# Two-tensor operations moved from GpSimd to VectorE in the dense part of a two-block kernel

## The chip, the cores and the metric

The kernel runs on one core of a Trainium2 chip. The metric is the time of one execution on the device in microseconds (us); lower is better. The core has a matrix engine (TensorE, PE in the profile, PEld its weight loads) and three element-wise engines: VectorE (DVE), ScalarE (ACT) and GpSimd (POOL). SyncE (SP) issues most of the transfers (DMA).

## What is computed

Two blocks over 256 tokens of 1024 features, in fp32. The first mixes stick-breaking attention with a state-space branch (S5), attends to a memory of 256 rows, and ends with a feed-forward net with a short convolution. The second mixes an mLSTM with a gated branch and ends with 32 routed experts and a last norm. What the change touches is the norm and the recurrence:

```python
def rms_norm(x, gain):
    y = xf * lax.rsqrt(jnp.mean(xf * xf, axis=-1, keepdims=True) + RMS_EPS)
    return y * gain

def s5_branch(u, a_re, a_im, log_dt, b_re, b_im, c_re, c_im, d_skip, w_glu, b_glu):
    lam_bar = jnp.exp(lam * dt)
    bu = jnp.einsum('gpc,bsgc->bsgp', b_bar, ug)
    _, states = lax.associative_scan(_linear_recurrence_combine, (decay, bu), axis=1)
    y = jnp.einsum('gcp,bsgp->bsgc', c_mat, states).real

h = rms_norm(x, norm_mix_pre)
proj = h @ w_in          # and so on: each dense stage is a norm and products with weights
```

## The kernel before, in words

**Weights.** `Stream` brings each weight matrix in units of 128x1024 elements (512 KB). SP issues the transfer into `wst` (five buffers), ScalarE copies the high part `whi` (L98), and `tick` forms the low part `wlo = wst - whi` on VectorE (L112) or, for the units listed in `gp` or `GU`, on GpSimd (L109). A product with full precision is three TensorE products: high by high, high by low, low by high. A unit makes 24 TensorE products of 256 columns (12 of 512) and four pairs of `whi` and `wlo` rotate.

**Norms.** `norm_by` multiplies the tokens by the gain (`xg`, L279, two pieces of 512), forms the reciprocal root in a chain of eight small VectorE operations on one column (`rs_v`, `rs_y`, `rs_t`, L228 to L238), and puts the root on a diagonal (`diag`, L282). TensorE transposes and scales in one step with it (`ax<-diag,xg`); ScalarE and VectorE split the result into `hT_hi` (L300) and `hT_lo` (L301). There are two tiles `t` of 128 tokens. At a change of stage `post_half` (sum `f`, L864), `post` and `hand_over` end one stage and begin the next with `norm_by`, and `yield_to` says behind which instruction the next units' low parts are ordered, and which of them go to GpSimd (`Y0`, `Y1`, `Y2`).

**State space.** `ssm_params` makes a table `s_T` of the powers of a rotation (cosines and sines) by doubling: on six levels, two products and two sums of growing length (L593, L595, L596), while the angles `s_P` are squared on VectorE (L599 to L601). Then `s_Bp` and `s_C` are built, and for each of four quarters `rotate` (L728 to L731) and `scan` (L737 to L742) run, between 85 and 170 us, with two GpSimd sums each.

**Order.** The program is written as Python that a scheduler orders, engine by engine. `issue_after(x)` puts an instruction behind `x` where both stand on one engine; `self.last["pool"]` is the last sum of the latest scan. At L1109 and L1117 the loads for the memory attention, and at L1314 those for the second block, are issued by GpSimd `behind("pool")`.

Of the kernel before, what the change touches and what calls it, by code (L numbers as in the profile page):

```python
# [14 lines left out]
OP = mybir.AluOpType  # L15
# [13 lines left out]
    return bass.AP(tensor=ap.tensor, offset=ap.offset, ap=[[0, 128], [1, n]])  # L29


GU = (40, 167, 171, 173)


class Stream:


    def __init__(self, k, pool, split, nb, ns, look):
        self.k, self.pool, self.nb, self.look = k, pool, nb, look
        self.plan, self.loaded, self.split, self.low, self.used = [], [], [], [], 0  # L40
        self.free, self.dmas = [], []
        self.limit, self.after, self.first, self.gp = 0, None, None, ()
        self.low_pool = split
        self.more(split, ns, 0)

    def yield_to(self, n, dve, act, pool=(), first=None):

        self.limit, self.after, self.first = self.used + n, (dve, act), first  # L50
        self.gp = [self.used + i for i in pool]

    def behind(self, i, j):
        x = self.first if i < self.limit and j == 0 else self.after and self.after[j]
# [49 lines left out]
    def tick(self):  # L104

        if self.low:
            i, lo, t, hi = self.low.pop(0)
            if i in self.gp or i in GU:
                self.k.nc.gpsimd.tensor_tensor(lo, t, hi, op=OP.subtract)  # L109
            else:  # L110
                with self.behind(i, 0):
                    self.k.nc.vector.tensor_tensor(lo, t, hi, op=OP.subtract)  # L112

    def next(self):
        while len(self.split) < min(len(self.plan), self.used + 1 + self.look):
            while len(self.loaded) <= len(self.split):
                while self.low and len(self.low) >= self.nb:
                    self.tick()
                self.fill()
            if not self._split():  # L120
                break
        self.used += 1
        while self.low and self.low[0][0] < self.used:
            self.tick()
        return self.split[self.used - 1]
# [5 lines left out]
def drive(*gens):  # L131

    gens = list(gens)
    while gens:
        for g in list(gens):
            if next(g, None) is None:
                gens.remove(g)
# [33 lines left out]
class K:  # L171
# [98 lines left out]
    def pair(self, pool):  # L270
        return pool.tile([128, 2], F32, name="ss2", tag="ss2", bufs=6)

    def norm_by(self, pool, t, ss, g, hi, lo, eng=None, dg=None):

        nc = self.nc
        xg = self.xn("xg")
        for n in range(2):
            ns = slice(n * 512, (n + 1) * 512)
            (eng or nc.vector).tensor_tensor(xg[:, ns], self.x[:, t, ns], g[:, ns], op=OP.mult)  # L279
        y = self.rsqrt(pool, ss[:, 0:1], None, ss2=ss[:, 1:2])  # L280
        dg = (dg or pool).tile([128, 128], F32, name="diag", tag="diag", bufs=1)
        self.last["diag"] = nc.vector.tensor_scalar(dg[:], self.ident[:], y[:], None, op0=OP.mult)  # L282
        return self.split_T(xg, hi, lo, t, dg)
# [170 lines left out]
            self.ws.add(w[k * 128:(k + kq) * 128, c0:c0 + ncols], kq, level)  # L454


Y0 = (1, 1)
Y1 = (4,(2,3))
Y2 = (5, (0, 3))


NWARM = 40
# [2 lines left out]
class Block1(K):  # L465
# [56 lines left out]
    def ssm_params(self, pool, work):  # L522
        nc = self.nc
        V, G, A = nc.vector, nc.gpsimd, nc.scalar
# [23 lines left out]
        r = work.tile([128, 16], F32, name="s_r")  # L548
# [32 lines left out]
        T = self.s_T = pool.tile([128, 2, 16, 64], F32, name="s_T")  # L581
# [5 lines left out]
        m4 = tg[:].rearrange("p j e i c -> p j (e i c)").rearrange("p j (a i n) -> p j a i n", a=2, i=16)  # L587
        pm = work.tile([128, 2, 16], F32, name="s_pm")
        for lv in range(8):
            if lv > 1:  # L590
                n = 1 << lv - 2
                for j in range(2):
                    G.tensor_tensor(m4[:, j, :, :, :n], T[:, :, :, :n],  # L593
                                    P[:, lv, j, :][:, None, :, None].to_broadcast([128, 2, 16, n]), op=OP.mult)
                G.tensor_tensor(T[:, 0, :, n:2 * n], m4[:, 0, 0, :, :n], m4[:, 1, 1, :, :n], op=OP.subtract)  # L595
                G.tensor_tensor(T[:, 1, :, n:2 * n], m4[:, 0, 1, :, :n], m4[:, 1, 0, :, :n], op=OP.add)  # L596
            if lv < 7:
                c, s = P[:, lv, 0, :], P[:, lv, 1, :]
                V.tensor_tensor(pm[:], P[:, lv], P[:, lv], op=OP.mult)  # L599
                V.tensor_tensor(P[:, lv + 1, 0, :], pm[:, 0], pm[:, 1], op=OP.subtract)  # L600
                V.scalar_tensor_tensor(P[:, lv + 1, 1, :], c, 2.0, s, op0=OP.mult, op1=OP.mult)  # L601
            yield 1
# [67 lines left out]
    def ssm_scan(self, pool, work, uT, y):  # L670


        nc = self.nc
        V, G, A = nc.vector, nc.gpsimd, nc.scalar
        Bp, C, T, R = self.s_Bp, self.s_C, self.s_T, self.s_R
# [44 lines left out]
        def cs(q):  # L720
            return [T[:, j, 4 * q:4 * q + 4, :].rearrange("p i j -> p (i j)")[:, None, :].to_broadcast([128, 2, 256])
                    for j in range(2)]

        def rotate(q):
            ec, es = cs(q)
            b = bu.pop(q)[:].rearrange("p (a n) -> p a n", a=2)
            m1, m2 = M[q] = [work.tile([128, 2, 256], F32, name=f"s_m{c}", tag=f"s_m{c}", bufs=2) for c in "12"]
            V.tensor_tensor(m1[:], b, ec, op=OP.mult)  # L728
            V.tensor_tensor(m2[:], b, es, op=OP.mult)
            G.tensor_tensor(m1[:, 0], m1[:, 0], m2[:, 1], op=OP.add)  # L730
            G.tensor_tensor(m1[:, 1], m1[:, 1], m2[:, 0], op=OP.subtract)  # L731

        def scan(q):
            ec, es = cs(q)
            m1, m2 = M[q]
            for j in range(2):
                V.tensor_tensor_scan(m2[:, j, :], R[:, 4 * q:4 * q + 4, :].rearrange("p i j -> p (i j)"), m1[:, j, :],  # L737
                                     0.0, op0=OP.mult, op1=OP.add)
            V.tensor_tensor(m1[:], m2[:], ec, op=OP.mult)
            V.tensor_tensor(m2[:], m2[:], es, op=OP.mult)  # L740
            G.tensor_tensor(m1[:, 0], m1[:, 0], m2[:, 1], op=OP.subtract)
            self.last["pool"] = G.tensor_tensor(m1[:, 1], m1[:, 1], m2[:, 0], op=OP.add)  # L742
            for g, h in enumerate(halves):
                A.activation(Cz[h, :, :, g, :], C[h, 1:5, :, 4 * q:4 * q + 4, :].rearrange("p e j i c -> p (e j) i c"),
                             AF.Copy)
# [129 lines left out]
            self.mean2(self.nw, self.x[:, t, ns], s2, n)  # L875
        return s2

    def hand_over(self, t, g, hh, hl, n, pool):

        r = self.norm_by(self.nw, t, self.post(t), g, hh, hl)  # L880
        if t == 0:
            self.diag0 = self.last["diag"]
        else:
            self.ws.yield_to(n, *r, pool, self.diag0)

    def new_h(self):
        return (self.hp.tile([128, 8, 256], F32R, name="hT_hi", tag="hT_hi"),
# [26 lines left out]
    def next_tile(self, t):  # L914
        self.post(t)
# [25 lines left out]
    def block1(self):  # L941
        nc, tc, I = self.nc, self.tc, self.I
        V, G, A = nc.vector, nc.gpsimd, nc.scalar
        c, nw, ws = self.const, self.nw, self.ws
        if True:
# [15 lines left out]
            for nm, n in (("b_gate", 16), ("ssm_d", 4), ("ssm_b_glu", 4)):  # L961
                r = rows[nm] = self.rowp.tile([64, 128], F32, name=f"r_{nm}")
# [17 lines left out]
            hh, hl = self.new_h()  # L980
            for t in range(2):
                ss = self.pair(nw)
                for n in range(2):
                    self.mean2(nw, self.x[:, t, n * 512:(n + 1) * 512], ss, n)
                with self.behind("diag" if t else "const"):
                    r = self.norm_by(nw, t, ss, g, hh, hl, G if t else None, sw if t else None)
            ws.yield_to(Y0[0], *r, range(Y0[1]))

            gT = p1.tile([128, 16, 256], F32, name="gT")
            uT = p1.tile([128, 4, 256], F32, name="uT")  # L990
# [51 lines left out]
            with ExitStack() as s2:  # L1042
                self.banks(3, 0)
                sw = s2.enter_context(tc.tile_pool(name="ssm_work", bufs=1, reuse_waits="tile"))
                a, b = self.stick(nw, qT, kT, v, oh, ol), self.ssm_scan(sp, sw, uT, uT)
# [74 lines left out]
            hh, hl = self.new_h()  # L1120
# [6 lines left out]
            gx = self.gain("norm_xa_pre")  # L1127
# [7 lines left out]
            gp, gx = self.gain("norm_xa_post"), self.gain("norm_ffn_pre")  # L1135
# [50 lines left out]
            oxh, oxl = meh, mel  # L1186
            for h in range(4):
                po = self.bank()
                for dk in range(2):
                    for mt in range(2):  # L1190
# [6 lines left out]
                                op=OP.subtract)  # L1197
            hh, hl = self.new_h()

            drive(self.mode_a(oxh, oxl, 8, 1024, lambda t, b: self.hand_over(t, gx, hh, hl, *Y1), tail=8,  # L1200
                              half=lambda t, n, b: self.post_half(t, n, b, gp)))
            xst.close()

# [1 line left out]
            with tc.tile_pool(name="ffn", bufs=1, reuse_waits="tile") as fp:  # L1205
# [32 lines left out]
                for b in range(6):  # L1238
                    n = 512 if b < 5 else 256
# [8 lines left out]
class Block2(Block1):  # L1248
# [47 lines left out]
        self.h2 = self.new_h()  # L1296

    def next_tile(self, t):
        self.hand_over(t, self.g1, *self.h2, *Y2)

    def plan2(self):
        win = self.I["w_in_2"][0]
# [750 lines left out]
```

## Time and profile before

| | us |
|---|---|
| three runs | 1132.81, 1136.93, 1130.77 |
| their median | 1132.81 |
| the profiled execution | 1129.9 |
| its span, first to last instruction | 1128.2 |
| its mean granted TensorE clock | 0.986 of full speed |
| busy: TensorE, VectorE, ScalarE, GpSimd | 1071.8, 562.6, 439.2, 112.6 |

The dense part (first block, mixer of the second) lasts until some 676 us, then the experts follow. In the rows below a window's columns are its length, the busy time and count of PE, PEld, DVE, ACT and POOL, the granted clock, the share of the 16 DMA engines that moved data, and GB/s. A clock of 0.50 is 1.2 GHz, 1.00 is 2.4 GHz.

### The profile page before, as it was taken

Reading aid. Unit: us, or ns where it says so; the run is one execution under the profiler, and the core shown is the slowest. Engines: PE = TensorE matmul, PEld = TensorE weight load, DVE = VectorE, ACT = ScalarE, POOL = GpSimd, SP = SyncE. Lnnn points to the kernel's source line nnn. Section 1 sums busy time; section 2 is a strip of 40 time slices with the busy share of each in tenths; the row PEclk is TensorE's granted clock in tenths of the full one; section 3 lists DMA queues with packets and bytes.
Section 4 is the critical chain, followed back from the end, with each engine's and each line's share of the span. In section 5 each row is a group of like instructions: output and inputs, shape, how many; then the busy total and the mean of one; then the engine's idle time right before and its main releaser. Section 6 shows DMA issues by size and latency. Waiting matters only on the chain. (4 is left out here: it accounts for less than half of the span.)

```text
span 1128.2 us, 17920 instructions
## 1 busy us (share of the span) xinstructions
PE 1071.8 (95%) x6552; PEld 760.0 (67%) x6552; DVE 562.6 (50%) x1232; ACT 439.2 (39%) x703; POOL 112.6 (10%) x140
## 2 busy tenths in 40 slices
PE   7889999999999999999999879999999999999994
PEld 7878899899887999987798754434343444443332
DVE  8985446995447888855676982211111111211003
ACT  4454467565535766643478331111011101110102
POOL 3734142100002000000101020000000000000000
PEclk9989999999999999999999989999999999999998
DMA  7442255675516665662596676999999999999994
GB/s 225 148 155 91 77 161 182 219 267 162 153 53 222 228 188 171 196 192 80 171 326 239 217 295 246 341 409 409 408 409 409 408 409 372 409 409 408 409 407 157
DMA packets 103850, 294.36 MB, mean 261 GB/s; under 512 B 14733, under 2 KB 17009, under 8 KB 103761
## 3 DMA queue, kind: packets, MB, share of 16 engines
q1 hardware_dynamic: 101136, 286.33, 70.0%
q0 software_dynamic: 2336, 6.35, 1.9%
q8 instruction: 52, 0.85, 0.3%
q10 hardware_dynamic: 288, 0.52, 0.1%
q14 instruction: 38, 0.30, 0.1%
HBM read 304.70 MB, written 1.05 MB: 271 GB/s over the span
## 5 line engine op out<-in xcount | busy, mean ns | idle before, releaser
L112 DVE TENSOR_TENSOR wlo<-wst,whi 128x1024 fp32r<-128x1024 f32 x171 | 213.9, 1259 | 98.9 <-ACT whi L98 97.8
L98 ACT ACTIVATE whi<-wst 128x1024 fp32r<-128x1024 f32 x180 | 188.1, 1057 | 131.7 <-PE mm L194 116.3
L194 PE MATMUL mm<-hT_hi,wlo 128*128 128x256 f32 x672 | 190.3, 283 | 6.7 <-DVE wlo L112 6.7
L194 PE MATMUL mm<-hT_hi,whi 128*128 128x256 f32 x672 | 193.8, 289 | 0.0
L194 PE MATMUL mm<-hT_lo,whi 128*128 128x256 f32 x672 | 190.0, 283 | 0.0
L194 PEld LDWEIGHTS mm<-hT_hi,wlo 128*128 128x128 f32 x672 | 128.3, 191 | 7.1 <-DVE wlo L112 7.1
L194 PEld LDWEIGHTS mm<-hT_hi,whi 128*128 128x128 f32 x672 | 128.2, 191 | 1.7 <-issue 1.4
L194 PEld LDWEIGHTS mm<-hT_lo,whi 128*128 128x128 f32 x672 | 128.3, 191 | 0.2
L1683 DVE SCALAR_TENSOR_TENSOR hid<-gu,ws,hid 128x512 f32<-128x512 f32 x16 | 12.0, 751 | 228.3 <-PE gu L1677 228.3
L1691 ACT ACTIVATE hidT<-yd 128x512 f32<-128x512 f32 x16 | 9.6, 598 | 157.0 <-PE yd L207 157.0
L109 POOL TENSOR_TENSOR wlo<-wst,whi 128x1024 fp32r<-128x1024 f32 x9 | 22.5, 2506 | 365.8 <-DVE rs_y L238 175.2
L1711 DVE SCALAR_TENSOR_TENSOR ylo<-gu,ws,yhi 128x512 fp32r<-128x512 f32 x16 | 12.0, 751 | 89.2 <-ACT yhi L1710 89.2
L194 PE MATMUL mm<-whi,hT_hi 128*128 128x512 f32 x128 | 51.5, 410 | 2.8 <-DVE f L864 2.8
L194 PE MATMUL mm<-whi,hT_lo 128*128 128x512 f32 x128 | 51.3, 404 | 0.0
L194 PE MATMUL mm<-wlo,hT_hi 128*128 128x512 f32 x128 | 51.1, 403 | 0.0
L1682 ACT ACTIVATE hid<-gt,ws 128x512 f32<-128x512 f32 x16 | 11.0, 687 | 102.0 <-PE gt L1677 102.0
L1710 ACT ACTIVATE yhi<-gu,ws 128x512 fp32r<-128x512 f32 x16 | 11.0, 687 | 99.1 <-PE gu L1701 99.1
L1987 POOL TENSOR_TENSOR o<-o,go 128x512 f32<-128x512 f32 x2 | 2.5, 1265 | 448.6 <-ACT o L1986 448.6
L1677 PE MATMUL gu<-xr,x 128*64 128x512 f32 x112 | 38.3, 596 | 1.4 <-DMA xr<-in_w_up_dram 1.4
L1677 PE MATMUL gu<-ra,x 128*64 128x512 f32 x140 | 35.3, 597 | 0.8 <-DMA ra<-in_w_up_dram 0.6
L194 PE MATMUL mm<-whi,ah 128*128 128x512 f32 x88 | 34.8, 396 | 0.0
L194 PE MATMUL mm<-wlo,ah 128*128 128x512 f32 x88 | 34.8, 395 | 0.0
(607 smaller groups left out, 2288.1 us busy)
## 6 DMA issues: line engine op xcount, KB each, us to landing
wst<-in_w_in_dram SPq DMA_DIRECT2D x56, 512.0 KB, 4.6
wst<-in_ffn_w_up_dram SPq DMA_DIRECT2D x44, 512.0 KB, 4.5
ra<-in_w_gate_dram SPq DMA_DIRECT2D x35, 512.0 KB, 9.9
ra<-in_w_up_dram SPq DMA_DIRECT2D x35, 512.0 KB, 10.1
ra<-in_w_down_dram SPq DMA_DIRECT2D x30, 512.0 KB, 10.1
xr<-in_w_up_dram SPq DMA_DIRECT2D x28, 512.0 KB, 7.0
xr<-in_w_down_dram SPq DMA_DIRECT2D x26, 512.0 KB, 10.1
xr<-in_w_gate_dram SPq DMA_DIRECT2D x24, 512.0 KB, 10.1
```

The costliest lines, as they stand in the source:

```text
L98: nc.scalar.activation(hi[:, :m], t[:, :m], AF.Copy)
L109: self.k.nc.gpsimd.tensor_tensor(lo, t, hi, op=OP.subtract)
L112: self.k.nc.vector.tensor_tensor(lo, t, hi, op=OP.subtract)
L194: i = self.nc.tensor.matmul(out, lhsT=lhsT, rhs=rhs, start=start, stop=stop, skip_group_check=True)
L1677: self.nc.tensor.matmul(ps[r, :], lhsT=xe[:, k, e], rhs=w[g][k], start=k == 0, stop=k == 7, skip_group_check=True)
L1682: self.nc.scalar.activation(hid[:], ps_g[:], AF.Silu, scale=y)
L1683: self.nc.vector.scalar_tensor_tensor(hid[:], ps_u[:], y, hid[:], op0=OP.mult, op1=OP.mult)
L1691: self.nc.scalar.activation(hT[:].rearrange("p a b -> p (a b)"), ps[:], AF.Copy)
L1710: self.nc.scalar.activation(hi[:], ps[n][:], AF.Copy, scale=ws)
L1711: self.nc.vector.scalar_tensor_tensor(lo[:], ps[n][:], ws, hi[:].bitcast(F32), op0=OP.mult, op1=OP.subtract)
L1987: G.tensor_tensor(o[1, n][:], o[1, n][:], self.go[:, ns], op=OP.mult)
```

## The change

Every two-tensor operation that GpSimd did in the dense part stands on VectorE: the gain product of the second tile in the first norm (2), the products and sums of the rotation table (24), the sums of `rotate` and `scan` (16), and nine low parts, one in the first norm, two each at two stage changes, four by `GU`. The arithmetic is the same.

```diff
-GU = (40, 167, 171, 173)
...
-    def yield_to(self, n, dve, act, pool=(), first=None):
+    def yield_to(self, n, dve, act, first):
         self.limit, self.after, self.first = self.used + n, (dve, act), first
-        self.gp = [self.used + i for i in pool]
...
             i, lo, t, hi = self.low.pop(0)
-            if i in self.gp or i in GU:
-                self.k.nc.gpsimd.tensor_tensor(lo, t, hi, op=OP.subtract)
-            else:
-                with self.behind(i, 0):
-                    self.k.nc.vector.tensor_tensor(lo, t, hi, op=OP.subtract)
+            with self.behind(i, 0):
+                self.k.nc.vector.tensor_tensor(lo, t, hi, op=OP.subtract)
...
-    def norm_by(self, pool, t, ss, g, hi, lo, eng=None, dg=None):
+    def norm_by(self, pool, t, ss, g, hi, lo, dg=None):
...
-            (eng or nc.vector).tensor_tensor(xg[:, ns], self.x[:, t, ns], g[:, ns], op=OP.mult)
+            nc.vector.tensor_tensor(xg[:, ns], self.x[:, t, ns], g[:, ns], op=OP.mult)
...
-Y0 = (1, 1)
-Y1 = (4,(2,3))
-Y2 = (5, (0, 3))
+Y0, Y1, Y2 = 1, 4, 5
...
                 for j in range(2):
-                    G.tensor_tensor(m4[:, j, :, :, :n], T[:, :, :, :n],
+                    V.tensor_tensor(m4[:, j, :, :, :n], T[:, :, :, :n],
                                     P[:, lv, j, :][:, None, :, None].to_broadcast([128, 2, 16, n]), op=OP.mult)
-                G.tensor_tensor(T[:, 0, :, n:2 * n], m4[:, 0, 0, :, :n], m4[:, 1, 1, :, :n], op=OP.subtract)
-                G.tensor_tensor(T[:, 1, :, n:2 * n], m4[:, 0, 1, :, :n], m4[:, 1, 0, :, :n], op=OP.add)
+                V.tensor_tensor(T[:, 0, :, n:2 * n], m4[:, 0, 0, :, :n], m4[:, 1, 1, :, :n], op=OP.subtract)
+                V.tensor_tensor(T[:, 1, :, n:2 * n], m4[:, 0, 1, :, :n], m4[:, 1, 0, :, :n], op=OP.add)
...
-            G.tensor_tensor(m1[:, 0], m1[:, 0], m2[:, 1], op=OP.add)
-            G.tensor_tensor(m1[:, 1], m1[:, 1], m2[:, 0], op=OP.subtract)
+            V.tensor_tensor(m1[:, 0], m1[:, 0], m2[:, 1], op=OP.add)
+            V.tensor_tensor(m1[:, 1], m1[:, 1], m2[:, 0], op=OP.subtract)
...
-            G.tensor_tensor(m1[:, 0], m1[:, 0], m2[:, 1], op=OP.subtract)
-            self.last["pool"] = G.tensor_tensor(m1[:, 1], m1[:, 1], m2[:, 0], op=OP.add)
+            V.tensor_tensor(m1[:, 0], m1[:, 0], m2[:, 1], op=OP.subtract)
+            self.last["pool"] = V.tensor_tensor(m1[:, 1], m1[:, 1], m2[:, 0], op=OP.add)
...
-    def hand_over(self, t, g, hh, hl, n, pool):
+    def hand_over(self, t, g, hh, hl, n):
...
-            self.ws.yield_to(n, *r, pool, self.diag0)
+            self.ws.yield_to(n, *r, self.diag0)
...
-                    r = self.norm_by(nw, t, ss, g, hh, hl, G if t else None, sw if t else None)
-            ws.yield_to(Y0[0], *r, range(Y0[1]))
+                    r = self.norm_by(nw, t, ss, g, hh, hl, sw if t else None)
+            ws.yield_to(Y0, *r, self.last["diag"])
```

The lines of the changed kernel have numbers lower by 8 to 10 (L112 is L104 there, L282 is L274, L301 is L293, L593 is L583, L864 is L854).

**The order at the start.** On VectorE, from the first tile's diagonal on, in the kernel before:

```order
L282 TENSOR_SCALAR diag<-ident,rs_y 128x128
L228 SCALAR_TENSOR_TENSOR rs_v<-ss_246 128x1
L229 TENSOR_SCALAR rs_y<-rs_v 128x1
L234 SCALAR_TENSOR_TENSOR rs_t<-rs_y,rs_v 128x1
L238 SCALAR_TENSOR_TENSOR rs_y<-rs_t,rs_y 128x1
L234 SCALAR_TENSOR_TENSOR rs_t<-rs_y,rs_v 128x1
L238 SCALAR_TENSOR_TENSOR rs_y<-rs_t,rs_y 128x1
L234 SCALAR_TENSOR_TENSOR rs_t<-rs_y,rs_v 128x1
L238 SCALAR_TENSOR_TENSOR rs_y<-rs_t,rs_y 128x1
L282 TENSOR_SCALAR diag<-ident,rs_y 128x128
L301 TENSOR_TENSOR hT_lo<-ax,hT_hi 128x4x128 x3
```

and in the changed kernel:

```order
L274 TENSOR_SCALAR diag<-ident,rs_y 128x128
L271 TENSOR_TENSOR xg<-x,gbc 128x512 x2
L220 SCALAR_TENSOR_TENSOR rs_v<-ss_246 128x1
L221 TENSOR_SCALAR rs_y<-rs_v 128x1
L226 SCALAR_TENSOR_TENSOR rs_t<-rs_y,rs_v 128x1
L230 SCALAR_TENSOR_TENSOR rs_y<-rs_t,rs_y 128x1
L226 SCALAR_TENSOR_TENSOR rs_t<-rs_y,rs_v 128x1
L293 TENSOR_TENSOR hT_lo<-ax,hT_hi 128x4x128
L230 SCALAR_TENSOR_TENSOR rs_y<-rs_t,rs_y 128x1
L226 SCALAR_TENSOR_TENSOR rs_t<-rs_y,rs_v 128x1
L293 TENSOR_TENSOR hT_lo<-ax,hT_hi 128x4x128
L230 SCALAR_TENSOR_TENSOR rs_y<-rs_t,rs_y 128x1
```

The second tile's two gain products stand behind the first diagonal now, and the first low part (`wlo_0_85`, a few rows further on, behind the second diagonal) ahead of the third `hT_lo`.

On GpSimd, from the IOTA that both have early, in the kernel before:

```order
L651 IOTA s_gi 128x8
L279 TENSOR_TENSOR xg<-x,gbc 128x512 x2
L109 TENSOR_TENSOR wlo_0_85<-wst,whi_0_84 128x1024
L538 COPY s_tv<-s_c 128x4x64 x4
L647 COPY s_R<-s_r_773 128x1024
L648 MEMSET s_R 128x16
L593 TENSOR_TENSOR s_tg<-s_T,s_P 128x32 x2
L595 TENSOR_TENSOR s_T<-s_tg 128x16
L596 TENSOR_TENSOR s_T<-s_tg 128x16
```

and in the changed kernel:

```order
L641 IOTA s_gi 128x8
L1251 DMA bif<-in_b_igate_dram 4x1
L1251 DMA bif<-in_b_fgate_dram 4x1
L459 DMA rows<-in_conv_qk_dram 8x128 x2
L320 DMA gbc<-in_norm_mem_dram 128x1024
L1815 DMA wr<-in_w_router_group_dram 128x8x4
L1816 DMA wr<-in_w_router_expert_dram 128x8x32
L1820 DMA brow<-in_b_router_group_dram 128x4 x2
L320 DMA gbc<-in_norm_mix_post_dram 128x1024
L1821 DMA brow<-in_b_router_expert_dram 128x32
L528 COPY s_tv<-s_c 128x4x64 x4
L637 COPY s_R<-s_r_773 128x1024
```

The loads that stood behind the last scan sum (in the trace of before at 152.5 us and later) stand ahead of the copies of `s_c` now, since that sum is on another engine.

**The order in the table.** On VectorE, from the end of the table to unit 12's low part (the `wlo` in the last row), in the kernel before:

```order
L112 TENSOR_TENSOR wlo_1_87<-wst,whi_1_86 128x1024
L662 TENSOR_TENSOR s_tv<-s_Bp,s_lam 128x512 x2
L667 TENSOR_TENSOR s_Bp<-s_tv 128x256 x2
L112 TENSOR_TENSOR wlo_2_89<-wst,whi_2_88 128x1024
L662 TENSOR_TENSOR s_tv<-s_Bp,s_lam 128x1024 x2
L112 TENSOR_TENSOR wlo_3_91<-wst,whi_3_90 128x1024
L667 TENSOR_TENSOR s_Bp<-s_tv 128x256 x4
L112 TENSOR_TENSOR wlo_0_85<-wst,whi_0_84 128x1024
```

and in the changed kernel:

```order
L104 TENSOR_TENSOR wlo_2_89<-wst,whi_2_88 128x1024
L624 TENSOR_TENSOR s_Bp<-s_Bp,s_tv 128x256
L625 TENSOR_TENSOR s_Bp<-s_Bp,s_tv 128x256
L104 TENSOR_TENSOR wlo_3_91<-wst,whi_3_90 128x1024
L652 TENSOR_TENSOR s_tv<-s_Bp,s_lam 128x512 x2
L1007 COPY bgate<-ax 128x16
L657 TENSOR_TENSOR s_Bp<-s_tv 128x256 x2
L1007 COPY dskip<-ax 128x4
L652 TENSOR_TENSOR s_tv<-s_Bp,s_lam 128x1024 x2
L1007 COPY bglu<-ax 128x4
L657 TENSOR_TENSOR s_Bp<-s_tv 128x256 x4
L104 TENSOR_TENSOR wlo_0_85<-wst,whi_0_84 128x1024
```

In the changed kernel the low parts of units 10 and 11 (`wlo_2_89`, `wlo_3_91`) stand ahead of the long products with `s_lam`, and that of unit 12 (`wlo_0_85`) behind all `s_Bp`. In the kernel before, units 10 and 11 stand between these products. The table's products and sums stand among the rows ahead of these.

**The order at the stage change at 532 us.** On VectorE, from the second tile's half of `f` on (L864, L854 in the changed kernel), in the kernel before:

```order
L238 SCALAR_TENSOR_TENSOR rs_y<-rs_t,rs_y 128x1
L282 TENSOR_SCALAR diag<-ident,rs_y 128x128
L112 TENSOR_TENSOR wlo_1_87<-wst,whi_1_86 128x1024
L112 TENSOR_TENSOR wlo_0_2313<-wst,whi_0_2312 128x1024
L301 TENSOR_TENSOR hT_lo<-ax,hT_hi 128x4x128 x2
L112 TENSOR_TENSOR wlo_2_2317<-wst,whi_2_2316 128x1024
L864 TENSOR_TENSOR f<-mm,gbc 128x512
L228 SCALAR_TENSOR_TENSOR rs_v<-ss_5604 128x1
L229 TENSOR_SCALAR rs_y<-rs_v 128x1
```

and in the changed kernel:

```order
L230 SCALAR_TENSOR_TENSOR rs_y<-rs_t,rs_y 128x1
L274 TENSOR_SCALAR diag<-ident,rs_y 128x128
L104 TENSOR_TENSOR wlo_0_85<-wst,whi_0_84 128x1024
L104 TENSOR_TENSOR wlo_1_87<-wst,whi_1_86 128x1024
L293 TENSOR_TENSOR hT_lo<-ax,hT_hi 128x4x128 x2
L104 TENSOR_TENSOR wlo_0_2313<-wst,whi_0_2312 128x1024
L104 TENSOR_TENSOR wlo_1_2315<-wst,whi_1_2314 128x1024
L854 TENSOR_TENSOR f<-mm,gbc 128x512
L220 SCALAR_TENSOR_TENSOR rs_v<-ss_5604 128x1
L104 TENSOR_TENSOR wlo_2_2317<-wst,whi_2_2316 128x1024
L221 TENSOR_SCALAR rs_y<-rs_v 128x1
```

Where two low parts stood between the diagonal and `hT_lo` and one behind, now two stand in each place, and a fifth behind `rs_v`.

## Rows read from the trace of the kernel before

**Rows 1.** Page, part 1: busy us (share of the span) xinstructions of each engine.
```profile
PE 1071.8 (95%) x6552; PEld 760.0 (67%) x6552; DVE 562.6 (50%) x1232; ACT 439.2 (39%) x703; POOL 112.6 (10%) x140
```

**Rows 2.** Busy time by stretches of the span, core 0.
```profile
28.00:56.00 28.00, 25.06 (x213) 24.70 (x212) 27.86 (x87) 13.35 (x20) 20.90 (x25) 1.00 0.46 148
60.00:66.00 6.00, 5.25 (x23) 5.20 (x24) 6.00 (x10) 1.88 (x5) 4.23 (x5) 0.50 0.56 170
544.00:546.00 2.00, 2.00 (x6) 1.52 (x5) 1.89 (x6) 0.60 (x2) 0.00 (x0) 0.50 0.89 305
676.00:682.00 6.00, 4.73 (x36) 4.55 (x36) 3.60 (x20) 2.85 (x14) 0.00 (x0) 0.92 0.00 0
```

**Rows 3.** Groups by shape on DVE, 169 to 190 us, where GpSimd does nothing.
```profile
L112 DVE TENSOR_TENSOR wlo<-wst,whi 128x1024 fp32r<-128x1024 f32 x6 | 7.2, 1222 | 3.8 <-ACT whi L98 3.8
L1074 DVE TENSOR_TENSOR mg<-mm,gT 128x256 f32<-128x256 f32 x4 | 1.4, 418 | 4.4 <-ACT gT L1071 4.4
...
L234 DVE SCALAR_TENSOR_TENSOR rs_t<-rs_y,rs_v 128x1 f32<-128x1 f32 x3 | 0.7, 221 | 0.1
```

**Rows 4.** Timeline of the start: start, length, instruction, [idle before <-releaser].
```profile
9.57 2.48 POOL L279 TENSOR_TENSOR xg<-x,gbc 128x512 f32<-128x512 f32 x2 [6.13 <-DMA x<-in_x_dram]
9.61 1.24 DVE L234 SCALAR_TENSOR_TENSOR rs_t<-rs_y,rs_v 128x1 f32<-128x1 f32 x1
...
10.88 1.19 DVE L238 SCALAR_TENSOR_TENSOR rs_y<-rs_t,rs_y 128x1 f32<-128x1 f32 x1
...
12.02 2.34 POOL L109 TENSOR_TENSOR wlo<-wst,whi 128x1024 fp32r<-128x1024 f32 x1
12.11 2.27 DVE L234 SCALAR_TENSOR_TENSOR rs_t<-rs_y,rs_v 128x1 f32<-128x1 f32 x1
...
15.39 5.17 PE L194 MATMUL ax<-diag,xg 128*128 128x128 f32 x32 [5.75 <-DVE diag L282]
```

**Rows 5.** Timeline of the rotation table: DVE and POOL.
```profile
35.41 0.53 POOL L593 TENSOR_TENSOR s_tg<-s_T,s_P 128x32 f32<-128x32 f32 x2 [2.71 <-DVE s_P L601]
...
50.36 4.83 POOL L593 TENSOR_TENSOR s_tg<-s_T,s_P 128x1024 f32<-128x1024 f32 x2
...
50.48 2.93 DVE L112 TENSOR_TENSOR wlo<-wst,whi 128x1024 fp32r<-128x1024 f32 x1
...
53.33 5.16 DVE L662 TENSOR_TENSOR s_tv<-s_Bp,s_lam 128x1024 f32<-128x1024 f32 x2
...
61.95 1.22 DVE L112 TENSOR_TENSOR wlo<-wst,whi 128x1024 fp32r<-128x1024 f32 x1
```

**Rows 6.** Timeline of TensorE: where units 10, 11 and 12 begin or wait.
```profile
53.47 0.38 PE L194 MATMUL mm<-hT_hi,wlo 128*128 128x256 f32 x1 [2.94 <-DVE wlo L112]
...
60.74 0.58 PE L194 MATMUL mm<-hT_hi,wlo 128*128 128x256 f32 x1 [3.71 <-DVE wlo L112]
...
65.61 0.58 PE L194 MATMUL mm<-whi,hT_hi 128*128 128x512 f32 x1
```

**Rows 7.** Timeline of the stage change at 532 us: DVE, POOL and PE.
```profile
532.17 2.40 DVE L234 SCALAR_TENSOR_TENSOR rs_t<-rs_y,rs_v 128x1 f32<-128x1 f32 x1
...
532.20 2.36 POOL L109 TENSOR_TENSOR wlo<-wst,whi 128x1024 fp32r<-128x1024 f32 x1 [175.16 <-DVE rs_y L238]
...
535.14 2.05 PE L194 MATMUL ax<-diag,xg 128*128 128x128 f32 x16 [2.28 <-DVE diag L282]
...
539.76 2.55 DVE L112 TENSOR_TENSOR wlo<-wst,whi 128x1024 fp32r<-128x1024 f32 x1 [1.20 <-ACT whi L98]
...
542.97 0.50 PE L194 MATMUL mm<-whi,hT_hi 128*128 128x512 f32 x1 [2.77 <-DVE f L864]
```

**Rows 8.** Timeline inside the mLSTM: DVE and PE.
```profile
624.84 2.44 DVE L236 TENSOR_TENSOR rs_t<-rs_y 128x4 f32<-128x4 f32 x2
...
628.73 0.30 PE L207 MATMUL ax<-ident,so 128*128 128x128 f32 x1 [1.61 <-DVE so L1405]
```

**Rows 9.** DMA queues, 152 to 163 us: packets, MB, share of 16 engines.
```profile
q0 software_dynamic: 591, 1.23, 43.3%
```

More of the change, by code (lines that the diff above doesn't have):

```diff
@@ L41, in __init__ @@
         self.free, self.dmas = [], []
-        self.limit, self.after, self.first, self.gp = 0, None, None, ()
+        self.limit, self.after, self.first = 0, None, None
         self.low_pool = split
         self.more(split, ns, 0)
-    def yield_to(self, n, dve, act, pool=(), first=None):
+    def yield_to(self, n, dve, act, first):
         self.limit, self.after, self.first = self.used + n, (dve, act), first
-        self.gp = [self.used + i for i in pool]
     def behind(self, i, j):
@@ L1198, in block1 @@
             hh, hl = self.new_h()
-            drive(self.mode_a(oxh, oxl, 8, 1024, lambda t, b: self.hand_over(t, gx, hh, hl, *Y1), tail=8,
+            drive(self.mode_a(oxh, oxl, 8, 1024, lambda t, b: self.hand_over(t, gx, hh, hl, Y1), tail=8,
                               half=lambda t, n, b: self.post_half(t, n, b, gp)))
@@ L1298, in next_tile @@
     def next_tile(self, t):
-        self.hand_over(t, self.g1, *self.h2, *Y2)
+        self.hand_over(t, self.g1, *self.h2, Y2)
     def plan2(self):
```

## The prediction

> **What bounds the kernel now.** I read the page's first part, then the busy time by stretches, then the timeline at each stretch where TensorE stands idle. TensorE is busy 1071.8 of 1128.2 us and GpSimd 112.6 [rows 1]: the sum over the whole span says only that TensorE leads, so the change is worth what TensorE's pauses ahead of the experts are worth. The stretches [rows 2] (length; busy time of PE, PEld, DVE, ACT, POOL, each with its count; granted clock; DMA share; GB/s) show where these lie. From 28 to 56 us VectorE is busy 27.86 of 28 and GpSimd 20.90, while TensorE has 25.06. From 676 to 682 the DMA share is 0.00: the stream of expert weights starts afresh there, released by the routing behind the dense part, so what the dense part gains should reach the end.
>
> Undisturbed, a low part of 128x1024 takes VectorE 1222 ns, a two-input operation of 128x256 418 ns, one step of the root 221 ns [rows 3]. Through two points that is 0.15 us and 1.05 ns for each element, and the next one starts some 0.08 us before the end of the one ahead (my estimate from starts in the timeline).
>
> **Part one, the start.** While GpSimd multiplies the second tile's gain from 9.57 and forms the first low part from 12.02, VectorE's root steps of one element for each partition take 1.24 and 2.27 us where 0.22 is usual; TensorE stands 5.75 us for the diagonal [rows 4]. These two steps and the one of 1.19 us between them hold an excess of 1.02 + 2.05 + 1.0 = 4.1 us. Without GpSimd the diagonal comes so much earlier. VectorE gets two products of 128x512 (0.61 us each) and one low part (1.14) instead, 2.4 us; they stand behind the first diagonal, and the first tile's products (half of 5.17 us) cover all but some 0.9. Best case: 3.2 us.
>
> The order shows a side effect. The DMA issues that GpSimd held back behind its last scan sum now stand right behind `s_gi`, some 150 us earlier, at about 3.4. In the stretch 152 to 163 us this queue moved 1.23 MB and took 43.3% of the 16 engines for 11 us [rows 9], which is 4.8 us of all engines. At the start these engines are filled with `x`, the gain and the first weights. If all of it lands ahead of what TensorE waits for, more than the 3.2 is gone; but the second large row waits for VectorE's second gain product, and the small ones behind it, so rather a third to a half counts. I take a gain of 1.7 and keep 0 to 3.2.
>
> **Part two, the rotation table.** Here 24 operations move. Their sizes are 2 x (32+64+...+1024) for the products and 2 x (16+...+512) for the sums, 6048 elements in all: 6048 x 1.05 ns + 24 x 0.07 us = 8.0 us on VectorE [rows 3]. Each reads what the one ahead wrote, and I add 1 us for that, and 0.3 us for three copies that now stand ahead: 9.3.
>
> Against it stands what VectorE loses to GpSimd. From 35.41, where the table begins, to the end of unit 12's low part (61.95 + 1.22 = 63.17) [rows 5] it executes, by the order, 26 operations of 16 or 32 elements, 4 of 512, 8 of 256 and 8 of 1024, one behind the other. Undisturbed these are 26 x 0.085 + 4 x 0.61 + 8 x 0.34 + 8 x 1.14 = 16.5 us; it took 27.8. The excess of 11.3 us lies in rows such as the low part of 2.93 us, and 5.16 us for two products whose undisturbed time is 2.4, under two GpSimd products of 4.83 [rows 5]. So the low part of unit 12 ends at 63.17 - 11.3 + 9.3 = 61.2, and with the start 59.5.
>
> Is it the shared way to SBUF? The rows show VectorE slowed and GpSimd too. The Trainium skill (SBUF — State Buffer, section Who interferes with whom) goes further: a VectorE instruction with two SBUF inputs and a GpSimd instruction that reads SBUF exclude each other for the whole instruction. By that rule VectorE would lose nearly all of GpSimd's time in the table, about 20 us rather than 11, and the change would free twice as much. The trace agrees at the root steps and not here, where VectorE finished a low part and half a product under GpSimd's two; I go by the 11.3.
>
> For TensorE: it now waits 2.94 us for unit 10's low part and 3.71 for unit 11's, and then runs at half clock (granted 0.50 from 60 to 66) [rows 2, 6], so unit 12 starts at 65.61 and not at 63.5. After the change units 10 and 11 have their low parts ahead of most of the `s_Bp` work, and unit 12 behind it. From unit 10's low part to unit 12's there are 8.8 us of VectorE work, so unit 10's ends at 50.7. TensorE would be there at 50.5 - 1.7 = 48.8, waits 1.9, is through unit 11 at 56.4, and waits 3.1 for unit 12 at 59.5. That is 6.1 us ahead of 65.61; if this pause brings the low clock as the one of 3.71 did, 2 us less. **I take 4.5 us for parts one and two; bounds 0 (start gains nothing, half the excess stays, clock drops) and 7.5.**
>
> **Part three, the stage change at 532 us.** A root step takes 2.40 us beside GpSimd's low part of 2.36, and TensorE waits 2.28 for the diagonal; then a low part of 2.55 us on VectorE stands ahead of the sum `f` beside GpSimd's second, and TensorE waits 2.77 for `f` [rows 7], and has the low clock (0.50) from 544 to 546 [rows 2]. After the change no GpSimd work is there. The two low parts stand on VectorE behind the diagonal (order below) and cost 2.3 us. The diagonal then comes 2.2 us earlier, and its wait goes. `f` is queued behind four low parts, two before and two behind `hT_lo`, and the last two must wait for ScalarE's high parts; it starts at about 538.8 rather than 542.3, and TensorE, which is there at 542.97 - 2.77 - 2.2 = 538.0, waits 1.5 rather than 2.77. The low clock cost some 8 products 0.19 us each (starts in the timeline), 1.5 us, and a pause of 1.5 should not bring it. Sum 2.2 + 1.2 + 1.5 = 4.9; if ScalarE delays the last low part by more, or the clock falls all the same, 2.2. **I take 4.8, bounds 2.2 and 5.5.**
>
> **Part four, the rest.** At 628.73 TensorE waits 1.61 us for VectorE's `so`, just after two root steps of 2.44 us beside GpSimd [rows 8]; these fall back to 0.2, and of the two low parts that VectorE gets for it (2.3 us) one lies earlier: **1 us, bounds -1 and 2**. The 16 rotation and scan sums (0.34 us each, 5.4 in all) go to VectorE between 85 and 170 us, in which it is idle over half of the time; each chain gets shorter, since GpSimd took over 0.7 us for each and a hand-over. Low parts at 193, 339 and 596 us lie where TensorE did not wait for them. **0, bounds -1 and 1.**
>
> **Sum.** 4.5 + 4.8 + 1 = 10.3 us off the profiled execution's 1129.9 (span 1128.2 and 1.7 around it) is 1119.6. The median of the three runs, 1132.8, is 2.9 above that execution, so I forecast 1122 for a median.
>
> **Rivals.**
> *VectorE becomes the bound (slower).* It is full in the table already, gets 9.3 us there, and TensorE waits for its low parts. If the long rows were VectorE's own chain of dependent small operations, unit 12's low part would come at 63.17 + 9.3 = 72.5, 6.9 us behind 65.61, and with the clock and 1 us at each of two stage changes it is +9 to +11: 1143. It decides once less than about 6 of the 11.3 us vanish. Against it: the long rows are long for single instructions of a known size, and only beside GpSimd. The Trainium skill (Perfetto Trace Analysis, section Optimizing Scalar/DVE Operations) advises giving work away from a saturated VectorE, which would speak against this change, and adds that GpSimd may not help because of the shared port. The trace bears out the second half: 2.40 us beside 2.36. Chance 0.07.
>
> *The early DMAs eat the gain.* If they delay `x`, the first weights and then `s_c` by the full 4.8 us, the start loses 1.6 instead of gaining 1.7, and TensorE's transposes of `s_tv` come late: parts one and two give 0 to 1, the sum is some 5, the median 1128. For it: the engines are full then. Chance 0.16.
>
> *The experts swallow it.* Their weights stream at full DMA load to the end; if that stream's start is fixed by loads and not by routing, the time stays at 1131 to 1133. Against it: the 0.00 from 676 to 682 [rows 2]. Chance 0.05.
>
> **How the numbers follow.** The forecast has 0.72. Its own range is 1129.9 less 15.5 (all upper bounds) to less 5, with the 2.9: 1117 to 1128. For 8 in 10 I add the early DMAs and part of the swallowed case: 1115 to 1130. About 0.5% (5.7 us) is what a measurement here can tell from no change. Faster than 1127.1: nearly all of the forecast and a little of the second rival, 0.74; same: most of the second and the third, 0.19; slower: 0.07.
>
> **What would show it.** In the changed kernel's profile no root step longer than 0.3 us at 9 to 16 and 532; VectorE's low parts at 36 to 62 back to 1.22 us; TensorE's first product at 17 to 20 us instead of 20.4, its wait for unit 11 gone and one of about 3 us at unit 12; at the stage change no wait for the diagonal and at most 1.5 for `f`. Wrong would be: first product after 20.4 (DMAs), VectorE rows that stay long without GpSimd, a wait at unit 12 of over 6 us, or a routing that ends 10 us earlier while the last store does not.

## The result and the profile after

The changed kernel takes 1116.5 us (median of 4 runs, 1115.6 to 1118.7) against 1131.8 before: a ratio of 0.9864, 95% interval 0.9841 to 0.9887. Run once more later, beside other kernels, it had 0.989 (0.9869 to 0.991). It is faster by 12 to 15 us; the forecast was 1122 with a range of 1115 to 1130, and a gain of 10.3 us. Since the changed kernel's own ratio moved by 0.003 from the first group of runs to the last, differences of 2 to 3 us between kernels of different groups below rest on their traces, and those within a group on the times too. Two traces of the changed kernel itself agree within 0.2 us from 62 to 180 us and lie 2.1 to 2.8 us apart from 270 us on, so a difference of that size late in a trace shows nothing by itself.

The page's first part, in the columns of [rows 1]:

```profile
PE 1068.7 (96%) x6552; PEld 756.5 (68%) x6552; DVE 565.6 (51%) x1283; ACT 438.7 (39%) x703; POOL 54.6 (5%) x89
```

GpSimd lost 58 us of busy time and VectorE gained 3. The work that moved is more than 3 us on VectorE; what it no longer loses beside GpSimd makes up for the rest. The stretch that had 27.86 us of VectorE and 20.90 of GpSimd [rows 2] shows it:

```profile
28.00:56.00 28.00, 24.04 (x182) 23.69 (x181) 26.21 (x106) 13.87 (x21) 2.12 (x3) 0.88 0.53 182
```

VectorE executes 106 instructions instead of 87 there. Nearly all of the 1.8 us in which it is idle are a wait for weights (below); behind that it is as full as before, 25.91 of 26 us from 36 to 62. TensorE has less than before (24.04 against 25.06), at a mean clock of 0.88: a new pause lies in this stretch (below).

Where the time came from is read by comparing the start of the same TensorE instruction in both traces; the difference is what has been gained up to there.

| TensorE instruction | before | after | gained |
|---|---|---|---|
| first product with weights | 20.36 | 17.26 | 3.1 |
| unit 12, first product with a low part | 66.02 | 62.08 | 3.9 |
| first product behind the state space's first block | 87.32 | 81.53 | 5.8 |
| behind the second wait for `uT` | 129.92 | 122.72 | 7.2 |
| second tile's transposes, stage change at 532 | 535.14 | 525.67 | 9.5 |
| first product of the next stage | 542.97 | 532.29 | 10.7 |
| the same stage, at full clock again | 547.41 | 535.19 | 12.2 |
| experts, a transpose at 697 us | 697.26 | 683.80 | 13.5 |
| end of the span | 1128.2 | 1114.0 | 14.2 |

**The start**, in the timeline (start, length, instruction, idle before and its releaser), answers to [rows 4]:

```profile
10.04 0.22 DVE L226 SCALAR_TENSOR_TENSOR rs_t<-rs_y,rs_v 128x1 f32<-128x1 f32 x1
...
10.94 0.28 DVE L274 TENSOR_SCALAR diag<-ident,rs_y 128x128 f32<-128x128 f32 x1
...
11.28 2.05 PE L186 MATMUL ax<-diag,xg 128*128 128x128 f32 x16 [2.08 <-DVE diag L274]
...
15.44 2.02 PE L186 MATMUL ax<-diag,xg 128*128 128x128 f32 x16 [2.11 <-DVE diag L274]
...
28.63 1.06 ACT L93 ACTIVATE whi<-wst 128x1024 fp32r<-128x1024 f32 x1 [5.85 <-DMA wst<-in_w_in_dram]
...
29.72 1.23 DVE L104 TENSOR_TENSOR wlo<-wst,whi 128x1024 fp32r<-128x1024 f32 x1 [4.13 <-ACT whi L93]
```

The root steps are back at 0.22 us and the diagonal is there at 10.94 instead of 15.05. TensorE then waits 2.11 us for the second diagonal (forecast 0.9), and the clock makes up for that: its 32 transposes take 4.1 us, and took 5.17 before, where the granted clock from 15 to 20 us was 0.68. The last two rows show what the late loads below prove to be the price of GpSimd's early loads: the weights of unit 5 land late, ScalarE waits 5.85 us for them and VectorE 4.13.

**The table and unit 12**, timeline, beside [rows 5, 6]:

```profile
45.53 2.34 DVE L583 TENSOR_TENSOR s_tg<-s_T,s_P 128x1024 f32<-128x1024 f32 x2
...
47.89 1.21 DVE L104 TENSOR_TENSOR wlo<-wst,whi 128x1024 fp32r<-128x1024 f32 x1
...
49.15 0.58 PE L186 MATMUL mm<-hT_hi,wlo 128*128 128x256 f32 x1 [3.96 <-DVE wlo L104]
...
62.08 0.50 PE L186 MATMUL mm<-wlo,hT_hi 128*128 128x512 f32 x1 [0.87 <-DVE wlo L104]
```

The low part takes 1.21 us, the two longest products 2.34 (forecast at the rate of 1.05 ns an element: 2.3). But the 4.13 us in which VectorE had no weights come back as a wait of 3.96 at unit 9. It stands where the forecast had no wait, and the one forecast at unit 12 is 0.87 and not 3.1.

**The stage change** at 532 us, timeline, beside [rows 7]:

```profile
525.33 0.29 DVE L274 TENSOR_SCALAR diag<-ident,rs_y 128x128 f32<-128x128 f32 x1
525.53 2.36 DVE L104 TENSOR_TENSOR wlo<-wst,whi 128x1024 fp32r<-128x1024 f32 x2
...
531.55 0.69 DVE L854 TENSOR_TENSOR f<-mm,gbc 128x512 f32<-128x512 f32 x1 [0.20 <-ACT sq L260]
...
532.29 0.50 PE L186 MATMUL mm<-whi,hT_hi 128*128 128x512 f32 x1 [1.56 <-DVE f L854]
```

No wait for the diagonal, 1.56 us for `f` (forecast 1.5), and no low clock behind it (granted 1.00 from 532 to 538).

### The profile page after: what moved, and what is told of

Its sections match the earlier page's. It is cut to its first block, busy times and chain, and to the rows that moved or that the text cites. A ratio compares the mean times of both kernels' runs of the same rounds, so it can differ in the third digit from the quotient of the medians.

```text
span 1114.0 us, 17908 instructions
## 1 busy us (share of the span) xinstructions
PE 1068.7 (96%) x6552; PEld 756.5 (68%) x6552; DVE 565.6 (51%) x1283; ACT 438.7 (39%) x703; POOL 54.6 (5%) x89
## 3 DMA queue, kind: packets, MB, share of 16 engines
HBM read 304.70 MB, written 1.05 MB: 274 GB/s over the span
## 5 line engine op out<-in xcount | busy, mean ns | idle before, releaser
L104 DVE TENSOR_TENSOR wlo<-wst,whi 128x1024 fp32r<-128x1024 f32 x180 | 220.5, 1235 | 98.0 <-ACT whi L93 97.2
L186 PE MATMUL mm<-whi,al 128*128 128x512 f32 x88 | 34.7, 396 | 0.0
L1667 PE MATMUL gt<-ra,x 128*64 128x512 f32 x140 | 33.5, 596 | 0.6 <-DMA ra<-in_w_gate_dram 0.6
```

The source lines that it names most:

```text
L186: i = self.nc.tensor.matmul(out, lhsT=lhsT, rhs=rhs, start=start, stop=stop, skip_group_check=True)
L1667: self.nc.tensor.matmul(ps[r, :], lhsT=xe[:, k, e], rhs=w[g][k], start=k == 0, stop=k == 7, skip_group_check=True)
```

## The experiments

Ratios are to the kernel before, from runs on the same chip. The first four ran as one group, the next four as a second, the last three as a third.

**Late loads.** Is the early issue of GpSimd's loads a cost, and how large?

```diff
-            self.last["pool"] = V.tensor_tensor(m1[:, 1], m1[:, 1], m2[:, 0], op=OP.add)
+            V.tensor_tensor(m1[:, 1], m1[:, 1], m2[:, 0], op=OP.add)
...
-                G.tensor_copy(um[h, :, r, :], ...)
+                self.last["pool"] = G.tensor_copy(um[h, :, r, :], ...)
```

> The changed kernel, but GpSimd's loads for the memory attention and the second block stay behind a GpSimd copy of the last quarter of the scan, as late as in the kernel before. Theory A (VectorE gains by GpSimd's silence, and the early loads are a cost): unit 5's weights land some 4 us earlier, VectorE no longer stands idle 4.13 us ahead of that low part, TensorE's wait of 3.96 us at unit 9 and the low clock behind it go; 3 to 6 us below the changed kernel, 1110 to 1114. Rival B (the early loads are part of the gain, since they no longer run beside weights at 152 us): the gain shrinks, 1117 to 1121. Rival C (they don't matter): 1116 to 1117.

Measured: 1119.9 us, 0.9893 (0.9871 to 0.9914), above the changed kernel's first 0.9864 and level with its second 0.989. The total lies in rival B's range; the trace does not speak for it. Unit 12's first low product is at 59.10, 3.0 us earlier than in the changed kernel, as theory A says. Then that gain is lost in one place, and TensorE is 1.7 us behind the changed kernel at 85 us. It stays 1.7 behind up to 200 us, so the loads that run beside weights at 152 us cost nothing there. The timeline on GpSimd, VectorE and TensorE, and the busy time by stretches (in the columns of [rows 2]):

```profile
58.93 14.89 POOL L677 COPY s_Bz<-s_Bp 64x512 f32<-64x512 f32 x1
...
73.26 0.56 DVE L807 SCALAR_TENSOR_TENSOR at<-az,at 128x384 f32<-128x384 f32 x1
...
75.48 0.90 PE L199 MATMUL sb<-ident,s_Bz 128*128 128x128 f32 x3 [3.15 <-POOL s_Bz L677]
```

```profile
76.00:78.00 2.00, 2.00 (x9) 1.91 (x8) 0.00 (x0) 1.11 (x2) 1.84 (x4) 0.50 0.81 212
58.00:74.00 16.00, 13.24 (x64) 10.88 (x64) 16.00 (x25) 8.04 (x13) 15.92 (x3) 1.00 0.60 198
```

A copy that takes GpSimd 1.6 us in the changed kernel (and 0.7 in a later quarter) took 14.89. Through these 16 us VectorE was busy without a gap, and its rows there have their undisturbed lengths (a low part 1.22 us). GpSimd came through only when VectorE's row of operations with two inputs in SBUF broke off: the copy ends at 73.82, with the operation of 0.56 us that reads one of its two inputs (`az`, which TensorE writes) from PSUM. TensorE waited 3.15 us for it, and its clock fell to 0.50 behind the wait.

**The sums back on GpSimd.**

```diff
-            V.tensor_tensor(m2[:], m2[:], es, op=OP.mult)
-            V.tensor_tensor(m1[:, 0], m1[:, 0], m2[:, 1], op=OP.subtract)
-            self.last["pool"] = V.tensor_tensor(m1[:, 1], m1[:, 1], m2[:, 0], op=OP.add)
+            self.last["pool"] = V.tensor_tensor(m2[:], m2[:], es, op=OP.mult)
+            G.tensor_tensor(m1[:, 0], m1[:, 0], m2[:, 1], op=OP.subtract)
+            G.tensor_tensor(m1[:, 1], m1[:, 1], m2[:, 0], op=OP.add)
...  (and the two sums of rotate)
```

> The changed kernel with the 16 sums of rotate and scan on GpSimd again, and the loads left early. Theory A: TensorE's two waits for uT come back (0.5 and 0.75 us, with what they move 1.4), the wait of 1.5 for the transposed block does not, since it hung on s_Bp: 1117.5 to 1118.5. Rival (all that was gained between 66 and 130 us, 3.3 us, is due to these sums): 1119.5 to 1120.5. Rival (hidden): 1116.5.

Measured: 1119.6 us, 0.9883 (0.9862 to 0.9905), between the changed kernel's two ratios, so the total tells nothing. What TensorE waited for between 60 and 170 us in its profiled execution (total, times, longest):

```profile
PE sb L199 <- POOL s_Bz L677: 3.2, 1, 3.2
PE mm L186 <- DVE wlo L104: 1.8, 1, 1.8
PE yq L702 <- DVE uT L748: 1.3, 2, 0.8
```

The two waits for `uT` are back and cost 1.4 us in the trace, as theory A has it. The first row is the shut-out copy again (14.90 us); this execution took 1124.4 and the three others 1118.6 to 1120.0. That suits a copy that is shut out in some executions of one kernel and not in others, but the three have no trace, so it is not shown.

**The table back on GpSimd**, alone and on the best version below.

```diff
-                    V.tensor_tensor(m4[:, j, :, :, :n], T[:, :, :, :n],
+                    G.tensor_tensor(m4[:, j, :, :, :n], T[:, :, :, :n],
...  (and the two sums below)
```

> The changed kernel with the 24 products and sums of the rotation table on GpSimd again. Theory A (what VectorE loses beside GpSimd is more than the work it takes over): VectorE's rows at 36 to 62 us are long again, unit 12 starts 2 to 5 us later and the wait for the transposed block (1.5) comes back: 1119 to 1124. Rival B (the 3.96 us wait at unit 9 is VectorE's own work, so the table is better off on GpSimd): 1112 to 1116.

Measured: 1126.6 us, 0.9947 (0.9929 to 0.9966), 6.5 to 9 us above the changed kernel by its two ratios, and 8.8 in the trace at 82 us, more than theory A expected; rival B is out. VectorE's low part for unit 12 starts 2.5 us later, and TensorE's first product with it 4.5 us later. TensorE's waits from 28 to 100 us:

```profile
PE mm L186 <- DVE wlo L104: 8.5, 4, 4.4
PE sb L186 <- ACT s_BT L688: 2.3, 1, 2.3
```

**The low parts alone**, moved in the kernel before.

```diff
-GU = (40, 167, 171, 173)
+GU = ()
...
-Y1 = (4,(2,3))
-Y2 = (5, (0, 3))
+Y1 = (4,())
+Y2 = (5, ())
```

> The kernel before with only the eight later low parts on VectorE (units 40, 167, 171, 173 and those of the two stage changes); start, table and sums stay on GpSimd. Theory A: the waits for the diagonal (2.28) and for f (2.77 to 1.5) and the low clock (1.5) at 532 us go, and 1 us in the mLSTM: 6 us below before, 1125 to 1127. Rival (the gain at 532 comes from the shifted arrival of weights, not from GpSimd): 1129 to 1132.

Measured: 1127.6 us, 0.994 (0.9914 to 0.9965): 6 to 7 us off. Between 525 and 560 us one wait of TensorE is left, the same as in the changed kernel:

```profile
PE mm L194 <- DVE f L864: 1.6, 1, 1.6
```

Across the change TensorE gains 4.9 us on the kernel before, as much as in the changed kernel (2.9 us behind at 530 us, 2.0 ahead at 549). So the gain at 532 us needs nothing of the other parts.

**Late loads, and the first quarter's copies on ScalarE.** If the copy that was shut out ate the gain of the late loads, taking it off GpSimd gives it back.

```diff
+                cp = (lambda o, i: A.activation(o, i, AF.Copy)) if q == 0 else G.tensor_copy
-                G.tensor_copy(Bz[h, :, :, g, :], Bp[...])
+                cp(Bz[h, :, :, g, :], Bp[...])
...
-                self.last["pool"] = G.tensor_copy(um[h, :, r, :], uT[...])
+                self.last["pool"] = cp(um[h, :, r, :], uT[...])
```

> The kernel with late loads, and the first quarter's copies of s_Bp and uT (two of 64x512, four of 32x256) on ScalarE instead of GpSimd. Theory A2 (with late loads GpSimd's copy of 14.89 us was shut out by VectorE's unbroken two-input operations, and TensorE's wait of 3.15 us for s_Bz with the low clock behind it ate the gain of 3 us): the wait goes and the gain stays, 3 us below the changed kernel's ratio, 0.983 to 0.985, 1113 to 1115. Rival (the late loads themselves cost it, at 150 us): 0.989, as with late loads alone.

Measured: 1114.6 us, 0.9832 (0.9802 to 0.9862). TensorE's waits from 28 to 100 us:

```profile
PE mm L186 <- DVE wlo L104: 3.1, 2, 2.2
```

The wait for `s_Bz` is gone and the 3 us are kept: unit 12's first low product at 58.99, and still 3.1 us ahead of the changed kernel at 155 us.

**The start back on GpSimd**, in that version (gain products of the second tile and first low part).

> The kernel above with the second tile's gain products and the first low part on GpSimd again. Theory A: the first root's steps take 1.2 to 2.3 us again and TensorE begins 3 us later; 2.5 to 3.5 us above the kernel above. Rival (later waits for low parts swallow the start): less than 1 us above.

Measured: 1115.8 us, 0.9857 (0.9825 to 0.989), 1.2 us above by the medians. The root step beside GpSimd is at 2.26 us again and the first product 3.3 us later, as theory A says. But only 2.0 of this are left from 25 to 240 us. Behind that it is 1.0 to 1.3, and 0.4 at 700, where one pair of traces tells nothing. The intervals of the two ratios overlap, so what the start is worth at the end, 0 to 2 us, is not settled between theory and rival.

**The table back on GpSimd in that version.**

> The kernel with late loads and ScalarE copies, with the rotation table on GpSimd again. Theory A by the prediction's sum (11.3 us of loss against 9.3 of work): some 2 to 3 us above. Theory A2 (as the table put back into the changed kernel showed, TensorE waits twice more and drops its clock): 6 to 9 us above. Rival B (the table is better off on GpSimd once the loads are late): equal or below.

Measured: 1120.5 us, 0.9891 (0.9862 to 0.9919), 6 us above. TensorE's waits from 28 to 100 us:

```profile
PE mm L186 <- DVE wlo L104: 4.8, 2, 3.7
PE sb L186 <- ACT s_BT L689: 2.3, 1, 2.3
```

At unit 12 TensorE is 2.5 us later, near what the prediction's sum says; the wait for the transposed block then doubles it to 5.2 at 75 us and 5.3 at 90. VectorE's own low part for unit 12 starts 2.1 us later, although VectorE came to the table 0.8 us earlier here, so the table costs VectorE 2.8.

**Early loads alone**, in the kernel before (its `last["pool"]` put on a VectorE operation).

> The kernel before, with only the order of GpSimd's loads changed: they stand at the start, as in the changed kernel, and all work stays where it was. Theory A (early loads delay the weights of unit 5): 2 to 5 us above before, 1134 to 1137. Rival (they cost nothing where VectorE is late anyway): within 1 us of before. Rival B (they are a gain): 1 to 3 us below.

Measured: 1132.2 us, 0.9997 (0.9977 to 1.0017): nothing. The loads cost 3.0 us at unit 12 in the changed kernel and nothing there (65.93 against 66.02), and 0.8 from 85 to 240 us, in a kernel where VectorE reaches its low parts late anyway.

**Once more, side by side**, and one more copy moved: `s_R`, 128x1024, to ScalarE.

```diff
-        G.tensor_copy(R[:], r4[:, :, None].to_broadcast([128, 16, 64]))
+        nc.scalar.activation(R[:], r4[:, :, None].to_broadcast([128, 16, 64]), AF.Copy)
```

> The changed kernel once more, on the chip of the next two, so that they are compared with it directly. Theory A: 0.985 to 0.988 of before, as the first time. Its trace shows whether GpSimd's copy of s_Bp is shut out here too (a wait of 3 us for s_Bz, as with the sums put back) or comes through, as in the first execution; theory A2 says that this is decided by a few tenths of a us and can go either way.

> Late loads and the first quarter's copies on ScalarE, once more. Theory A2: 2 to 3 us below the changed kernel (0.982 to 0.985 of before). Rival (the first difference of 0.003 was scatter between chips): within 1 us of the changed kernel.

> The kernel above with the copy of 128x1024 that fills s_R on ScalarE too. Beside it a low part takes 2.07 us instead of 1.22. Theory A: that row falls to 1.22, and what follows on VectorE is 0.8 us earlier up to unit 12; 0.5 to 0.9 us below the kernel above if ScalarE has room, which is at the edge of what can be told. Rival (a copy with one input does not keep VectorE out): the row stays at 2.07 and the time where it is.

Measured: the changed kernel 1119.2 us (1118.3 to 1120.1), 0.989; with late loads and ScalarE copies 1116.8 (1114.9 to 1118.5), 0.986 (0.9839 to 0.9881); with `s_R` too 1113.7 (1112.0 to 1117.2), 0.9842 (0.982 to 0.9864). The first two ratios are 0.001 above what was expected of them, and the third kernel lies further below the second than the 0.5 to 0.9 us expected. The second stays 2.4 us below the first (1114.6 against 1116.5 before, in two groups), though their slowest and fastest runs overlap, and every run of the third is below the fastest of the changed kernel's four beside it. In the changed kernel's second trace the copy took 1.6 us again, so there it was not shut out. The low part beside the copy of `s_R` is 2.07 us in the second kernel, with the copy on GpSimd, and without it:

```profile
29.20 1.22 DVE L104 TENSOR_TENSOR wlo<-wst,whi 128x1024 fp32r<-128x1024 f32 x1
```

What follows on VectorE gains 0.9 us by that row, as theory A says, and keeps it up to unit 12: VectorE is 1.5 us ahead of the second kernel's trace before the row and 2.3 at unit 12. The 1.5 are there from the first low parts on, ahead of `s_R`. The medians are 3.1 us apart, but the runs of the two overlap, and the size at the end is not settled. By its median this is the fastest version: the change, GpSimd's loads held back, and the copies on the path given to ScalarE.

## Why the prediction was right, and where its sum was off

**Start and table, 4.5 forecast, 3.9 measured at unit 12.** That the sum comes near is luck: two errors in its halves cancel. The start gave 3.1 us at the first product (1.7 forecast): the early loads did not delay `x` and the first weights. They delayed unit 5's, so the price of the loads fell on the table: 0.8 gained there, where 2.8 was forecast. With the loads late, unit 12 comes 3.0 us earlier. With the table back on GpSimd VectorE comes to unit 12's low part 2.7 and 2.8 us later in the two kernels, measured from where the table begins, against the sum's 11.3 less 9.3, which is 2.0. So the step that costed the table holds, a little low, and the step that placed the loads' cost at the start failed. The rival on the early loads was right that they cost time, and in part where: GpSimd's copies of `s_c` begin at 24.71 instead of 19.83, 4.9 us late. But `x` and the first weights, on which it let the start lose 1.6 us, were not late, and it was wrong that only 5 us would be left.

**The stage change, 4.8 forecast, 4.9 measured** (2.2 by the diagonal, 1.2 by `f`, 1.5 by the clock; 9.5 less 7.3 ahead of it, then 10.7 and 12.2). Moved alone, with the other low parts, it gave 6 to 7 us, where 4.8 + 1 were forecast.

**The rest, 1 forecast.** This is the term that was mis-sized. "0, bounds -1 and 1" for the sums and what lies around them was wrong by 3.3 us: 1.9 at the wait for the transposed block of the first quarter, and 1.4 at two waits for `uT`. The waits of TensorE from 60 to 170 us in the trace of before (total, times, longest) have both:

```profile
PE mm L194 <- DVE wlo L112: 3.7, 1, 3.7
PE sb L194 <- ACT s_BT L698: 1.5, 1, 1.5
PE yq L712 <- DVE uT L758: 1.3, 2, 0.7
```

In the changed kernel one is left there:

```profile
PE mm L186 <- DVE wlo L104: 0.9, 1, 0.9
```

Each of the two that are gone stands behind work that the change shortens. The first belongs to part two and not to the sums: the block is made from `s_Bp`, which comes behind the table, and part two followed the table only up to unit 12. The prediction argued from VectorE's idle share between 85 and 170 us and took no row of those waits. The two experiments with the table on GpSimd show the first (2.3 us), that with the sums the second.

The 1 us forecast for the mLSTM came out in size and not where it was placed: 1.3 us were gained between 547 and 697 us. TensorE's wait for `so`, 1.61 before [rows 8], is 0.6, but only 0.2 us more had been gained at 661 us than at 547. The kernel with only the low parts moved has the same wait of 0.6, and at 697 us 1.6 us are left of the 2.0 that it had gained at 549. The other 1.0 came in the routing, at 675 us of the kernel before, where TensorE was at the low clock for longer. The two windows begin at the same work, before and then after:

```profile
674.00:676.00 2.00, 2.00 (x6) 0.78 (x5) 0.76 (x4) 0.00 (x0) 0.00 (x0) 0.50 0.06 23
661.50:663.50 2.00, 2.00 (x10) 1.12 (x9) 1.21 (x7) 0.11 (x1) 0.00 (x0) 0.77 0.11 43
```

Why it was shorter is not shown. A last 0.7 us came among the experts; no experiment tells where from.

**The total.** The profiled execution came out 3.9 us below the sum's (14.2 gained on its span, 10.3 forecast). The median of the runs is 0.8 us above the profiled execution and not the 2.9 taken over from before, which makes up most of the rest of the 5.5 us between 1122 and 1116.5. The upper bounds add up to 16.0, not 15.5; the 14.2 lie within them.

**The rivals.** VectorE is still full in the table, and TensorE still waits there for its low parts (3.96 and 0.87 us). But the long rows were not its own: alone, they have the lengths that the sum used, and the table back on GpSimd costs 6 to 9 us. The experts swallowed nothing: 13.5 us ahead at 697, 14.2 at the end. The Trainium skill's advice against a saturated VectorE (Perfetto Trace Analysis, Optimizing Scalar/DVE Operations) fails here for the reason it gives itself, that GpSimd may not help; the measured 6 to 9 us stand for it.

**The shared way to SBUF.** The Trainium skill (SBUF — State Buffer, Who interferes with whom) says that the order of issue decides who blocks. The traces show losers on both sides: beside GpSimd's low part a VectorE step of 0.22 us took 2.40 [rows 7], and beside VectorE's unbroken row a GpSimd copy of 1.6 us took 14.89. The second does not fit that order: the copy began at 58.93, and more than 20 VectorE operations that began later went ahead of it. Nor is it shown that the rule fails in the table, as the prediction has it. Its 20 us are GpSimd's busy time there, and this holds waits of GpSimd's own: its sums of 128x512 took 2.15 and 2.24 us in the table, while a product of that size took 1.24 at the start [rows 4].

## What to carry to other kernels

Work given to GpSimd is not free because GpSimd is idle. Here VectorE's two-input operations beside the table lost more than it saved (2.0 us by the sum, 2.7 and 2.8 measured), and at the start and the stage change the loss fell on one-element steps on which TensorE waits. Before forecasting such a move, list every wait of the bounding engine behind the moved work, in each stage, and not the busy share of the engine that takes it. And look where the moved instruction's name is used to order other things: here it released eleven loads some 150 us earlier.

## What the runs showed that was not expected

A GpSimd copy was shut out for 14.89 us by a VectorE that ran two-input operations without a pause (rows above); in the trace of before it was VectorE that lost. It happened in two of the profiled executions, with late loads and with the sums back. In both traces of the changed kernel the same operations shared the time (copy 1.6 us, four low parts 5.45 instead of 4.6). What decides between the two is not shown.

In these rows a GpSimd operation that reads keeps VectorE out, and one that only writes does not. Beside GpSimd's copy of `s_R` with one input a low part took 2.07 us in the changed kernel. Beside its MEMSET of the same size one took 1.21, in the timeline of the changed kernel:

```profile
51.88 1.21 DVE L104 TENSOR_TENSOR wlo<-wst,whi 128x1024 fp32r<-128x1024 f32 x1
...
52.06 0.95 POOL L671 MEMSET s_Bz<- 128x1024 f32 x1 [17.79 <-DMA wst<-in_w_in_dram]
```
